# Turning round the two products of every second 128-column block in the channel-major units of a decoder layer

## The chip, the cores and the metric

The kernel runs on one core of one Trainium2 chip, in a single launch. The metric is the device time of one execution in microseconds (us), the median over several runs. The core's engines are named as in the profile: PE is TensorE (its matmuls, here also called products), PEld is TensorE's loading of the stationary operand, DVE is VectorE, ACT is ScalarE, POOL is GpSimd, and SP is SyncE, which issues the weight DMAs.

## What is computed

One decoder layer over 256 tokens of 2048 channels, in float32: half a SwiGLU feed-forward block (FFN1), a mixing stage (sparse attention beside a chunkwise mLSTM, gated and merged), and a second half block (FFN2). Cut to the parts that carry the products:

```python
def swiglu(x, w_gate, w_up, w_down):
    return (jax.nn.silu(x @ w_gate) * (x @ w_up)) @ w_down
...
        x = x + 0.5 * swiglu(rms_norm(x, ffn1_norm[l]), ffn1_w_gate[l], ffn1_w_up[l], ffn1_w_down[l])
        hn = rms_norm(x, mix_norm[l])
        proj = hn @ w_in[l] + b_in[l]
...
        merged = gates[..., :D_MODEL] * (o_nsa @ w_branch_nsa[l]) + gates[..., D_MODEL:] * (h_m @ w_branch_mlstm[l])
        x = x + merged @ w_out[l]
        x = x + 0.5 * swiglu(rms_norm(x, ffn2_norm[l]), ffn2_w_gate[l], ffn2_w_up[l], ffn2_w_down[l])
```

`w_gate` and `w_up` are 2048 x 5632, `w_down` is 5632 x 2048, `w_out` is 2048 x 2048, and the two branch weights are 1024 x 2048.

## The kernel before, in words

The weights stream through once. The program is a list of units (class `Unit`); each is a block of output columns of one weight matrix, cut into tiles of 1024 elements per partition (512 KB). Every tile is loaded by SP into `raw`, ACT casts it to `whi` (float32r, the high part), and DVE subtracts to leave `wlo` (the low part). Four buffers of each kind rotate (`NB = NRAW = 4`); the split of tile h + 3 is issued while tile h is being multiplied (the loop over `plan`, lines 1259 to 1284).

Activations are split likewise. In a channel-major unit (`unit_a`, line 353) the weights are stationary, and the activations of one block of 128 input channels, `a[:, kt]`, move: 256 tokens of the high part and 256 tokens of the low part side by side, 512 columns. For each block `kt` and each `c` of 128 output columns there are two products:

- the high product: `whi` against all 512 columns, into the whole bank `ps[:, c, :]` (line 363);
- the low product: `wlo` against the 256 high columns alone, added to the first half of the same bank (line 364).

A unit has 256 output columns, so `c` is 0 or 1, and a tile holds four `kt`. `kts` is the number of input blocks: 16 where the input has 2048 channels (`XX`, `M_`), 44 in the down projections (`H`), 8 in the branches (`O_`, `h_`). `fold` adds the two halves of the banks afterwards. There are 22 gate and 22 up units in each FFN, 8 and 7 down units in FFN1 and FFN2, and in mixing 24 units of 256 columns on `XX`, one of 128 columns (the gate tile, where `c` is only 0), 8 + 8 branch units and 8 of `w_out`.

Two other kinds of unit are not touched by the change: `unit_b` (token-major, all products of 512 columns, the trace's `mm<-whi,XX` and `mm<-wlo,XX`), and `unit_last` (the last 256 output columns of FFN2, all products of 256 columns). The two `cmp_unit` blocks (`sc<-whi,flat`, `sc<-wlo,flat`) have products of 256 columns as well, 16 in a row for a pair of tiles.

The order of the work on PE is written out by the program itself (a manual schedule): the order of calls is the order of the queue. `Estimate` keeps rough times, from which `step` decides where side work (attention, mLSTM, norms) goes in between the products; `mul` lets some small products of the side work in behind a product of the stream. In the trace nearly all operations carry line L110, that of the helper that passes calls on.

Of the kernel before, what the change touches and what calls it, by code (L numbers as in the profile page):

```python
# [31 lines left out]

# columns of the packed per-partition vectors
C_G1, C_GM, C_G2 = 0, 16, 32
# [11 lines left out]
class Unit:  # L46
    """A weight matrix block that runs through the tensor engine, tile by tile."""

# [5 lines left out]
class Estimate:  # L54
    """Rough times (us) at which the engines get through what they've been given so far, to tell when a
    piece of side work can go into the tensor engine's queue without holding it up."""
    TABLES = {AF.Exp: 1, AF.Silu: 2, AF.Sigmoid: 3, AF.Gelu_apprx_tanh: 4, AF.Ln: 5}
# [5 lines left out]
    def after(self, t):  # L63
        """What follows on the other engines depends on t, and in turn on itself."""
        self.at, self.by, self.end = t, None, t
# [30 lines left out]
class Engine:  # L96
    """Passes calls on, and counts them in the estimate; or keeps them for later (in kept)."""

# [16 lines left out]
def layer(ctx: ExitStack, tc: tile.TileContext, xt, cols, w_small, b_in,  # L115
# [22 lines left out]
    def side_bank(tag):  # L138
        """A bank for side work; free: the times its two banks are given back."""
        est.q["T"] = max(est.q["T"], free[tag].pop(0))  # L140
        held.append(tag)
        free[tag].append(1e9)
        return aux.tile([128, 512], F32, name=nm(tag), tag=tag, bufs=2)
# [4 lines left out]

    # ------------------------------------------------------------------ persistent tiles
    cl = per.tile([128, NCOL], F32, name="cl")  # L150
# [18 lines left out]

    # ------------------------------------------------------------------ helpers  # L170
    def rsqrt(o, ss, n, inv):
        """o = 1/sqrt(ss*inv + EPS), by Newton steps."""
        v = small(n, tag="rv", bufs=2)[0:o.shape[0]]
        t = small(n, tag="rt", bufs=2)[0:o.shape[0]]
        V.tensor_scalar(v, ss, inv, EPS, op0=OP.mult, op1=OP.add)
        V.tensor_scalar(t.bitcast(I32), v.bitcast(I32), 1, None, op0=OP.logical_shift_right)
        V.tensor_scalar(o.bitcast(I32), t.bitcast(I32), -1.0, float(0x5F3759DF), op0=OP.mult, op1=OP.add)
        for _ in range(3):
            V.scalar_tensor_tensor(t, o, -0.5, o, op0=OP.mult, op1=OP.mult)
            V.tensor_mul(t, t, v)  # L180
            V.scalar_tensor_tensor(o, t, 1.5, o, op0=OP.add, op1=OP.mult)

    cur = {}

    # Side work goes in jobs, and these in steps: products first (up to a yield), then what takes
    # them up (up to a yield, of the names of the jobs that have to be over before it goes on, or of the
    # time from which on it can).
    jobs, past = [], {}
# [27 lines left out]
    def step(forced=None):  # L216
        """Starts a step of a job, if one is due; those without products are done at once."""
        while jobs:
# [30 lines left out]
    def mul(*a, **k):  # L249
        """A product of the weight stream; some small ones of the side work go in behind it."""  # L250
        T.matmul(*a, **k)
        for _ in range(min(len(small_ones), 2 + len(small_ones) % 2)):
            small_ones.popleft()()

    def settle():
        """Takes up the small products that were spread over the last ones of the weight stream."""
        while small_ones:
            small_ones.popleft()()
        j, cur["late"] = cur.get("late"), None
        if j:  # L260
            uptake(j)
# [16 lines left out]

    # ------------------------------------------------------------------ weight stream
    tiles = []  # L280
# [54 lines left out]
    def blocks(w, c0, ncol, kts):  # L335
        """The tiles [128, nk, ncol] of 1024 elements per partition of w[:, c0:c0+ncol]."""
        nk = 1024 // ncol
        v = w.rearrange("(k p) n -> p k n", p=128)
        return [(v[:, k:k + nk, c0:c0 + ncol], nk, ncol) for k in range(0, kts, nk)]

    def unit_b(w, c0, H, L, kts, done, pre=None):
        """Token-major: out[tok, 512 columns], activations stationary."""
        def emit(ps, h, e, wh, wl):
# [9 lines left out]
    def unit_a(w, c0, ncol, kts, act, done, pre=None):  # L353
        """Channel-major: out[128 columns, tok] for each 128 of ncol columns, weights stationary."""
        nk = 1024 // ncol

        def emit(ps, h, e, wh, wl):
            a = act()
            for k in range(e * nk // 2, (e + 1) * nk // 2):
                kt = nk * h + k  # L360
                for c in range(ncol // 128):
                    cs = slice(c * 128, c * 128 + 128)
                    mul(ps[:, c, :], wh[:, k, cs], a[:, kt].rearrange("p a t -> p (a t)"), start=kt == 0, stop=False)
                    mul(ps[:, c, 0:S], wl[:, k, cs], a[:, kt, 0, :], start=False, stop=kt == kts - 1)
        return Unit(blocks(w, c0, ncol, kts), emit, done, pre)

    def unit_last(w, c0, ncol, kts, act, done):
        """As unit_a, but with one sum, and one 128 columns after the other at the end; done(ps, c) for each."""
        nk = 1024 // ncol
# [18 lines left out]
    def fold(o, ps, c=2):  # L388
        """Sum of the two halves that unit_a leaves."""
        A.copy(o, ps[:, 0:c, S:])  # L390
# [3 lines left out]

    # ------------------------------------------------------------------ residual stream pieces

    def g_r():
        """rstd of the residual: R per token, and RB along the free axis on each partition."""
        ps = psS()
# [17 lines left out]
    def residual(pool, c, ps, half, gcol, name):  # L417
        """Adds 256 channels to X; then scales and splits them for the next products."""
        y = pool.tile([128, 2, S], F32, name=nm("y"), tag="y", bufs=2)
# [32 lines left out]

    # ------------------------------------------------------------------ FFN
    def ffn(wg, wu, wd, first, nxt, name):
        """first: the job that leaves this norm's rstd; nxt: the next norm's gain column, or None for
        the last one (then it is stored); name: the job that leaves the next rstd."""
        env = {}
# [61 lines left out]

    # ------------------------------------------------------------------ mixing  # L520
    def mixing():
# [50 lines left out]

        # ---- gate tile: rows 0-3 forget, 32-35 input, 64-111 attention gates
        def gate_done(ps):
# [44 lines left out]

        # ---- compressed keys and values  # L620
        def kcvc_done(ps):
# [6 lines left out]
        def g_flat(kc, w):  # L628
            """The blocks' positions on the partitions, split; columns (part, group, block)."""
            tr = psT().rearrange("p (g t) -> p g t", g=2)  # L630
# [9 lines left out]
            for lp in range(2):  # L640
                o = slice(lp * 64, lp * 64 + 64)
                for gpar in range(2):
                    v = tr[gpar * 64:gpar * 64 + 64, :, lp:]
                    # token 16 * block + 2 * k + lp of group 2 * g + gpar
                    src = bass.AP(tensor=v.tensor, offset=v.offset, ap=[v.ap[0], [2, 16], [S, 2], [16, 15]])
# [70 lines left out]

        # ---- queries and keys, normalised
        def normed(src, dst, n):
            """src, dst [128, 2, 64*n/2]: each 64 columns divided by their rms."""
            yield  # L720
# [39 lines left out]
        def g_qt(q, g):  # L760
            """Of each head of the group, both parts of its queries, one below the other."""
            qs = env["q", g] = env["N"].tile([128, 4, S], F32R, name=nm("qs"), tag="qs", bufs=2)
# [15 lines left out]
        def g_kk(g):  # L778
            """The keys of the group (selected, window), split, each part on both halves of the partitions."""
            kk = env["k", g] = env["N"].tile([128, 2, 2, S], F32R, name=nm("kk"), tag="kk", bufs=2)  # L780
# [23 lines left out]

        # ---- attention
        def gates_of(g):
            """Attention gates of the group: [tok, tile, head, branch]."""
            return env["gat"].rearrange("p t (g r b) -> p t g r b", g=4, r=4)[:, :, g]
# [131 lines left out]

        # ---- mLSTM
        def mv_done(c):
# [149 lines left out]

        # ---- merge
        def sig_done(key, c):
# [103 lines left out]

    # ------------------------------------------------------------------ start
    nc.scalar.dma_start(cl, cols)  # L1200
# [55 lines left out]

    # ------------------------------------------------------------------ run
    banks = {}
# [87 lines left out]
```

## Time and profile before

| | us |
|---|---|
| median of 3 runs | 2255.24 (2254.92 to 2256.05) |
| span of the profiled execution, first to last instruction | 2240.6 |
| median less span: what lies around it | 14.6 |
| PE busy | 2228.4 (99%) |
| PEld busy | 1928.6 (86%) |
| DVE busy | 1370.9 (61%) |
| ACT busy | 1105.6 (49%) |
| HBM | 183 GB/s over the span |

The profile gives the profiled execution by its span alone; its 2240.6 us are set beside the median as they stand, and the 14.6 us around it are taken as the same for both kernels. A busy PE is not PE at its peak: a matmul's recorded duration overlaps the next one's. What a product costs is read from the distance between the starts of two products, or from the number of products in a stretch in which PE is never idle; this distance is called the pitch below.

### The profile page before, as it was taken

The page shows a single profiled execution, that of the slowest core. Times are in us where ns is not written, and L with a number is a line of the kernel's source. Part 1 is how long each engine was busy: PE and PEld are TensorE (multiplying, and loading weights), DVE is VectorE, ACT ScalarE, POOL GpSimd, SP SyncE. Part 2 cuts the span into 40 slices and gives each one's busy share as a digit, 9 for nine tenths or more (in the row PEclk, how much of TensorE's full clock was granted, in tenths as well). Part 3 has the DMA queues.
Part 4 walks back from the last instruction along what each step waited for, and adds up shares of the span by engine and source line. Part 5 has one row for each costly group of instructions (what it writes and reads, how often), then busy time and mean ns, then how long its engine had stood idle before and what let it go on. Part 6 is the DMA issues. An engine that isn't in the chain of part 4 may idle for free.

```text
span 2240.6 us, 31889 instructions
## 1 busy us (share of the span) xinstructions
PE 2228.4 (99%) x12685; PEld 1928.6 (86%) x12685; DVE 1370.9 (61%) x1711; ACT 1105.6 (49%) x1471; POOL 27.8 (1%) x54
## 2 busy tenths in 40 slices
PE   9999999999999999999999999999999999999999
PEld 7888888888888888778888888888888888888888
DVE  7656555555555677776766666665555555554553
ACT  6444444444444455566775544554444444443332
POOL 0000000000000000001100000000000000000000
PEclk9999999999999999999999999999999999999999
DMA  7666666666555676444556666655665556565663
GB/s 246 189 190 191 191 188 189 188 188 198 188 189 189 185 238 187 148 123 130 152 163 192 186 187 185 194 182 185 187 186 185 185 185 187 185 195 193 196 196 124
DMA packets 395078, 412.59 MB, mean 184 GB/s; under 512 B 13296, under 2 KB 375920, under 8 KB 394928
## 3 DMA queue, kind: packets, MB, share of 16 engines
q1 hardware_dynamic: 394064, 408.08, 58.9%
q0 software_dynamic: 720, 2.36, 0.4%
q8 instruction: 99, 1.62, 0.3%
q14 instruction: 51, 0.42, 0.1%
q10 hardware_dynamic: 144, 0.11, 0.0%
HBM read 408.40 MB, written 2.10 MB: 183 GB/s over the span
## 4 chain that ended last, share of the span: by engine, by line
PE 97%; DVE 1%; ACT 1%; DMA 1%; issue 0%; SPq 0%; DVEq 0%; ACTq 0%
PE mm L110 94%; PE sc L110 2%; PE tr L110 2%; DVE wlo L110 0%; DMA X<-in_xt_dram 0%; DMA raw<-in_w_in_dram 0%; DVE t L110 0%; DVE nx L110 0%; ACT whi L110 0%; ACT kk L110 0%; ACT t L110 0%; DVE y L110 0%; DVE kk L110 0%; ACT qs L110 0%; ACT XX L110 0%
## 5 line engine op out<-in xcount | busy, mean ns | idle before, releaser
L110 DVE TENSOR_TENSOR wlo<-raw,whi 128x1024 fp32r<-128x1024 f32 (+1 forms) x772 | 929.4, 1224 | 583.4 <-ACT whi L110 580.6
L110 PE MATMUL mm<-XX,whi 128*128 128x512 f32 x3600 | 1269.4, 397 | 4.8 <-DVE XX L110 4.8
L110 ACT CAST whi<-raw 128x1024 fp32r<-128x1024 f32 (+1 forms) x772 | 793.6, 1046 | 581.1 <-PE mm L110 450.1
L110 PE MATMUL mm<-XX,wlo 128*128 128x256 f32 x3600 | 1011.5, 281 | 0.9 <-DVE wlo L110 0.8
L110 PEld LDWEIGHTS mm<-XX,whi 128*128 128x128 f32 x3600 | 676.2, 188 | 165.0 <-ACT whi L110 5.8
L110 PEld LDWEIGHTS mm<-XX,wlo 128*128 128x128 f32 x3600 | 681.2, 189 | 2.7 <-DVE wlo L110 2.5
L110 PE MATMUL mm<-H,whi 128*128 128x512 f32 (+1 forms) x1496 | 493.6, 382 | 0.5 <-DVE y L110 0.5
L110 PE MATMUL mm<-H,wlo 128*128 128x256 f32 x1408 | 395.0, 281 | 0.0
L110 PEld LDWEIGHTS mm<-H,whi 128*128 128x128 f32 x1496 | 274.5, 188 | 58.6 <-DVE y L110 0.7
L110 PEld LDWEIGHTS mm<-H,wlo 128*128 128x128 f32 x1408 | 266.0, 189 | 0.0
L110 PE MATMUL mm<-whi,XX 128*128 128x512 f32 x576 | 192.3, 400 | 0.0
L110 PEld LDWEIGHTS mm<-whi,XX 128*128 128x128 f32 x576 | 108.2, 188 | 21.5 <-issue 0.7
L110 PE MATMUL mm<-wlo,XX 128*128 128x512 f32 x288 | 113.8, 395 | 0.2 <-DVE wlo L110 0.2
L110 PE MATMUL mm<-M__10731,whi 128*128 128x512 f32 x256 | 90.5, 397 | 0.0
L110 PE MATMUL mm<-M__10731,wlo 128*128 128x256 f32 x256 | 71.9, 281 | 0.0
L110 ACT COPY sg<-mm 128x512 f32<-128x512 f32 x44 | 25.8, 587 | 79.8 <-PE mm L110 79.8
L110 ACT COPY sh<-mm 128x512 f32<-128x512 f32 x44 | 25.8, 587 | 78.4 <-PE mm L110 78.4
L110 PEld LDWEIGHTS mm<-wlo,XX 128*128 128x128 f32 x288 | 54.3, 188 | 9.9 <-DVE wlo L110 0.6
L110 DVE TENSOR_TENSOR sg<-mm,sg 128x512 f32<-128x512 f32 x44 | 30.4, 692 | 50.6 <-ACT sg L110 50.5
L110 DVE TENSOR_TENSOR sh<-mm,sh 128x512 f32<-128x512 f32 x44 | 30.4, 692 | 50.2 <-ACT sh L110 50.2
L110 PEld LDWEIGHTS mm<-M__10731,whi 128*128 128x128 f32 x256 | 48.1, 188 | 11.9
L110 ACT CAST H<-sh 128x512 fp32r<-128x512 f32 x44 | 27.3, 621 | 62.1 <-DVE sh L110 62.1
(192 smaller groups left out, 1221.1 us busy)
## 6 DMA issues: line engine op xcount, KB each, us to landing
raw<-in_wu_dram SPq DMA_DIRECT2D x176, 512.0 KB, 4.7
raw<-in_wd_dram SPq DMA_DIRECT2D x176, 512.0 KB, 4.5
raw<-in_wg_dram SPq DMA_DIRECT2D x175, 512.0 KB, 4.7
raw<-in_w_in_dram SPq DMA_DIRECT2D x168, 512.0 KB, 4.4
raw<-in_w_out_dram SPq DMA_DIRECT2D x32, 512.0 KB, 4.5
raw<-in_wb_n_dram SPq DMA_DIRECT2D x16, 512.0 KB, 5.1
raw<-in_wb_m_dram SPq DMA_DIRECT2D x16, 512.0 KB, 4.4
bias<-in_b_in_dram POOLq DMA_DIRECT2D x9, 256.0 KB, 3.7
```

The lines of the kernel that those rows point to most:

```text
L110: return g(out, *a, **k)
```

## The change

In `unit_a`, for odd `c` and for all `kt` but the first and the last of a unit, the low product goes ahead of the high one. The products, their operands and banks are the same; only the order of the two is turned. (The change also drops comments.)

```diff
@@ -360,12 +360,17 @@
                 kt = nk * h + k
                 for c in range(ncol // 128):
                     cs = slice(c * 128, c * 128 + 128)
-                    mul(ps[:, c, :], wh[:, k, cs], a[:, kt].rearrange("p a t -> p (a t)"), start=kt == 0, stop=False)
-                    mul(ps[:, c, 0:S], wl[:, k, cs], a[:, kt, 0, :], start=False, stop=kt == kts - 1)
+                    both = a[:, kt].rearrange("p a t -> p (a t)")
+                    turn = c % 2 == 1 and 0 < kt < kts - 1
+                    if turn:
+                        mul(ps[:, c, 0:S], wl[:, k, cs], a[:, kt, 0, :], start=False, stop=False)
+                    mul(ps[:, c, :], wh[:, k, cs], both, start=kt == 0, stop=False)
+                    if not turn:
+                        mul(ps[:, c, 0:S], wl[:, k, cs], a[:, kt, 0, :], start=False, stop=kt == kts - 1)
         return Unit(blocks(w, c0, ncol, kts), emit, done, pre)
```

On PE, at the border between two tiles in the middle of a gate unit of FFN1 (`mm_380` is the pair of banks of the unit; `whi_362`, `wlo_363` are the old tile, `whi_391`, `wlo_392` the new one), the rows before are:

```order
L110 MATMUL mm_380<-XX,whi_362 128x512
L110 MATMUL mm_380<-XX,wlo_363 128x256
L110 MATMUL mm_380<-XX,whi_362 128x512
L110 MATMUL mm_380<-XX,wlo_363 128x256
L110 MATMUL mm_380<-XX,whi_391 128x512
L110 MATMUL mm_380<-XX,wlo_392 128x256
L110 MATMUL mm_380<-XX,whi_391 128x512
L110 MATMUL mm_380<-XX,wlo_392 128x256
```

and with the change, at the same place:

```order
L110 MATMUL mm_380<-XX,whi_362 128x512 x2
L110 MATMUL mm_380<-XX,wlo_363 128x256 x2
L110 MATMUL mm_380<-XX,whi_362 128x512
L110 MATMUL mm_380<-XX,whi_391 128x512
L110 MATMUL mm_380<-XX,wlo_392 128x256 x2
L110 MATMUL mm_380<-XX,whi_391 128x512 x2
```

The strict alternation of 512 and 256 columns has become two of 512 and two of 256 in turn; the old tile's last product is now one on `whi`, where it was one on `wlo`.

At the border between two units (`mm_482` is the next unit's pair of banks, and `sc_477` a small side product of a norm), the rows before are:

```order
L110 MATMUL mm_380<-XX,whi_391 128x512
L110 MATMUL mm_380<-XX,wlo_392 128x256
L110 MATMUL mm_380<-XX,whi_391 128x512
L110 MATMUL mm_380<-XX,wlo_392 128x256
L110 MATMUL mm_482<-XX,whi_416 128x512
L110 MATMUL sc_477<-ones,acc 128x2 x2
L110 MATMUL mm_482<-XX,wlo_417 128x256
```

and with the change:

```order
L110 MATMUL mm_380<-XX,wlo_392 128x256 x2
L110 MATMUL mm_380<-XX,whi_391 128x512 x2
L110 MATMUL mm_380<-XX,wlo_392 128x256
L110 MATMUL mm_380<-XX,whi_391 128x512
L110 MATMUL mm_380<-XX,wlo_392 128x256
L110 MATMUL mm_482<-XX,whi_416 128x512
L110 MATMUL sc_477<-ones,acc 128x2 x2
L110 MATMUL mm_482<-XX,wlo_417 128x256
```

The last `kt` of one unit and the first of the next keep the old order, four high and four low products that alternate; the side product sits where it sat. On DVE and ACT the sequence of instructions is unchanged.

## Rows read from the trace of the kernel before

**Rows 1.** The page, busy time by engine over the span.
```profile
PE 2228.4 (99%) x12685; PEld 1928.6 (86%) x12685; DVE 1370.9 (61%) x1711; ACT 1105.6 (49%) x1471; POOL 27.8 (1%) x54
```
**Rows 2.** Waits of PE, longest in total: us, times, longest.
```profile
PE mm L110 <- DVE XX L110: 4.8, 1, 4.8
PE mm L110 <- DVE wlo L110: 1.0, 3, 0.5
```
**Rows 3.** Costliest groups: out<-in, form, xcount | busy us, mean ns | idle before.
```profile
L110 PE MATMUL mm<-XX,whi 128*128 128x512 f32 x3600 | 1269.4, 397 | 4.8 <-DVE XX L110 4.8
...
L110 PE MATMUL mm<-H,wlo 128*128 128x256 f32 x1408 | 395.0, 281 | 0.0
```
**Rows 4.** Groups on PE from 60 to 700 us (FFN1).
```profile
L110 PE MATMUL mm<-XX,whi 128*128 128x512 f32 x1268 | 439.6, 391 | 0.0
...
L110 PE MATMUL mm<-H,whi 128*128 128x512 f32 x579 | 200.8, 391 | 0.0
```
**Rows 5.** Groups on PE from 1520 to 2190 us (FFN2).
```profile
L110 PE MATMUL mm<-XX,whi 128*128 128x512 f32 x1321 | 466.8, 399 | 0.0
...
L110 PE MATMUL mm<-H,whi 128*128 128x512 f32 x576 | 203.6, 399 | 0.0
```
**Rows 6.** Groups on PE from 1190 to 1490 us (end of mixing).
```profile
L110 PE MATMUL mm<-XX,whi 128*128 128x512 f32 x386 | 136.7, 399 | 0.0
...
L110 PE MATMUL mm<-M__10731,whi 128*128 128x512 f32 x256 | 90.5, 397 | 0.0
...
L110 PE MATMUL mm<-h__9138,whi 128*128 128x512 f32 x112 | 39.8, 397 | 0.0
L110 PE MATMUL mm<-O__6437,whi 128*128 128x512 f32 x96 | 34.2, 398 | 0.0
```
**Rows 7.** Stretches: busy us (count) of PE, PEld, DVE, ACT, POOL; clock, DMA.
```profile
60.00:700.00 640.00, 640.00 (x3694) 564.32 (x3693) 370.14 (x369) 293.79 (x336) 0.00 (x0) 1.00 0.61 190
1520.00:2190.00 670.00, 670.00 (x3794) 581.00 (x3793) 370.60 (x360) 294.42 (x327) 0.00 (x0) 1.00 0.60 189
```
**Rows 8.** Timeline of PE in a token-major unit: start us, length us, count.
```profile
760.24 0.62 PE L110 MATMUL mm<-whi,XX 128*128 128x512 f32 x2
...
766.37 0.39 PE L110 MATMUL mm<-whi,XX 128*128 128x512 f32 x1
766.60 0.39 PE L110 MATMUL mm<-XX,whi 128*128 128x512 f32 x1
```
**Rows 9.** Timeline of PE around 16 products of 256 columns (mixing).
```profile
803.33 0.39 PE L110 MATMUL mm<-whi,XX 128*128 128x512 f32 x1
803.56 0.28 PE L110 MATMUL sc<-whi,flat 128*128 128x256 f32 x1
803.67 0.28 PE L110 MATMUL sc<-wlo,flat 128*128 128x256 f32 x1
803.79 0.28 PE L110 MATMUL sc<-whi,flat 128*128 128x256 f32 x1
...
805.47 0.40 PE L110 MATMUL mm<-whi,XX 128*128 128x512 f32 x1
805.71 0.40 PE L110 MATMUL mm<-wlo,XX 128*128 128x512 f32 x1
805.94 0.62 PE L110 MATMUL mm<-whi,XX 128*128 128x512 f32 x2
```
**Rows 10.** Timeline of all engines in an up unit of FFN2.
```profile
1800.29 0.28 PE L110 MATMUL mm<-XX,wlo 128*128 128x256 f32 x1
1800.29 0.19 PEld L110 LDWEIGHTS mm<-XX,whi 128*128 128x128 f32 x1
1800.41 0.40 PE L110 MATMUL mm<-XX,whi 128*128 128x512 f32 x1
```
**Rows 11.** Timeline of ACT and DVE there: cast and subtraction of one tile.
```profile
1803.01 1.05 ACT L110 CAST whi<-raw 128x1024 fp32r<-128x1024 f32 x1 [1.77 <-PE mm L110]
...
1804.10 1.23 DVE L110 TENSOR_TENSOR wlo<-raw,whi 128x1024 fp32r<-128x1024 f32 x1 [1.59 <-ACT whi L110]
```

## The prediction

> **What bounds the kernel now.** I read the busy shares first: PE is busy 2228.4 of 2240.6 us, with 12685 products [rows 1]. Then PE's waits: the two longest entries come to 5.8 us in all, nearly all of it one wait at the start [rows 2]. So nothing else holds PE up, and no transfer or cast can be worth more than that. The time is the sum of the pitches of the products, and the question is what a pitch depends on.
>
> For that I count products in stretches where PE is busy for the whole stretch and the granted clock is 1.00 [rows 7]. One high and one low product make a pair. In FFN1, 640 us hold 1268 + 579 = 1847 pairs [rows 4]: 346.5 ns a pair. In FFN2, the same code, 670 us hold 1321 + 576 = 1897 pairs [rows 5]: 353.2 ns. At the end of mixing, 300 us hold 386 + 256 + 112 + 96 = 850 pairs [rows 6]: 352.9 ns. The reader is to see that the same alternation of 512 and 256 columns runs at two pitches 6.7 ns apart, steady over hundreds of us, with no wait, no change of the clock and the same load on the DMAs (190 and 189 GB/s [rows 7]). The longer pitch shows in the recorded length of the 512-column products too (399 against 391 ns [rows 4, 5]).
>
> Uniform runs show what the products cost without alternation. In a token-major unit 28 products of 512 columns lie between the starts 760.24 and 766.60 [rows 8]: 227.1 ns each. From 803.79 to 805.47, 14 products of 256 columns take 1.68 us [rows 9]: 120.0 ns each. Their sum, 347.1 ns, is the pitch of FFN1 within the reading. So **FFN1 runs as the uniform runs do, while FFN2 and most of mixing pay some 6.6 ns a pair on top**. That surplus is what an order of products can win; 0 is the most that it can win in FFN1, where it can only lose.
>
> **The change, part by part.** It adds and removes no product, load, cast or transfer; it moves low products ahead of high ones. I count what it turns. The pairs are 3600 on XX and, for H, the 1408 low products less 88 of the untouched last unit [rows 3], 256 on M [rows 6], and by the loops 128 each in the branches: 5432. A unit turns one pair in each input block but the first and last. The 88 gate and up units and 24 of mixing turn 14 each, 15 down units 42, 8 output units 14, 16 branch units 6: 1568 + 630 + 112 + 96 = 2406. Each turned pair makes a **group of four**, 512, 256, 256, 512: 952 groups in FFN1, 910 in FFN2 and 544 in mixing. A unit's other four pairs stay as they are.
>
> What a group costs today: 2 x 346.5 = 693.0 ns in FFN1, 2 x 353.2 = 706.4 in FFN2, 2 x 352.9 = 705.8 in mixing. What it will cost no row shows in a steady run, so I bound it. The lower end is 693.0, two pairs at FFN1's pitch; the uniform sum is near it, 2 x 227.1 + 2 x 120.0 = 694.2. The upper end is 706.4, FFN2's pitch. The nearest rows are the two switches of length around the 16 short products [rows 9]: the first two of 256 columns after a 512 take 803.79 - 803.56 = 0.23 us, and the first two of 512 after a 256 take 805.94 - 805.47 = 0.47 us, against 0.454 in the uniform run. Together 0.70 us, between the ends; but there each switch follows a long uniform run, and starts are read to 0.01 us. So 694 and 700 both fit; I take the middle, **697 ns**.
>
> By stage, against today: FFN1 952 x (697 - 693.0) = +3.8 us; FFN2 910 x (697 - 706.4) = -8.6 us; mixing 544 x (697 - 705.8) = -4.8 us. The pairs that keep their order at unit borders, four in each of 51 units of FFN2 and 48 of mixing, are 396; if half of them follow their neighbours to the short pitch, they give 198 x 6.5 ns = -1.3 us. The sum is **-10.9 us**, of the span's 2240.6 and likewise of the median, since I take the 14.6 us around the span as fixed: 2255.2 - 10.9 = 2244.3, rounded to 2244.
>
> What else moves. A tile's last reader of whi ends about one low product, 0.12 us, later relative to its neighbour on wlo, and wlo is free about 0.23 us earlier. The cast of a later tile waits for that buffer ("<- PE mm" [rows 11]). Cast and subtraction take 1.05 + 1.23 us [rows 11], and a tile lasts eight pairs, 2.8 us; the split runs three tiles ahead of its use. That leaves about 6 us, so 0.12 us costs nothing; were the cover gone, it would be 0.12 us for each of some 680 tiles, 80 us, and would show as PE waiting on DVE's wlo, 1.0 us today [rows 2]. What wlo is needed for first is unchanged, since the first product pair of a tile keeps its order. Side products sit where they sat, and ACT's and DVE's order is the same.
>
> A weight load starts with the product before its own: 1800.29 for both [rows 10]. So each load is covered by one product, and a 256-column product is the tight cover. In the old order and in the new, half the loads have this cover; that no load loses its cover is why I expect no large loss.
>
> [...]
>
> **The rivals.**
>
> *The order does nothing on balance.* Each stage keeps a pitch that comes from how the stream started after its last disturbance, or the group costs what the two switches add up to, 700 ns: FFN1 +6.7, FFN2 -5.8, mixing -3.2, borders -0.7: -3.0 us, 2252; with the pitches kept, 2255. For it: the same code has two pitches in one execution, so order alone does not decide. Against it: the uniform runs go back to 227.1 and 120.0 after side work, and the new order has two equal neighbours in each group. [...]
>
> *Two short covers in a row.* In the new order two loads in succession have only a 256-column product as cover, where before a 512-column one lay between them. If the surplus of FFN2 comes from the load behind a short product, and the two long products that follow do not take it up, each group pays it twice wherever it runs: 706.4 ns everywhere, so FFN1 loses 952 x 13.4 = +12.8 us, mixing 0.3, and FFN1's border pairs, 52 x 4 x 6.7 ns, 1.4: 2255.2 + 14.5 = 2270. For it: the 512 after a short product is the one that is drawn out, 805.71 - 805.47 = 0.24 us against 0.227. Against it: 14 short covers in a row run at 120.0 ns, without any surplus [rows 9]. Each ns of a group is worth 2406 x 1 ns = 2.4 us, so this case decides from about 703 ns a group on.
>
> *The best case* belongs to the forecast: 693.0 ns in every group, FFN2 -12.2, mixing -7.0, borders -2.6: -21.8 us, 2233.
>
> *The change does not take hold* can be left out: the order of PE's queue, written by hand, shows the groups.
>
> **How the numbers follow.** About 0.2%, 4.5 us, is what a measurement of this kernel can tell from no change. By the 2.4 us a ns, -4.5 us stands at a group of 699.6 ns and +4.5 us at 703.3. The forecast, groups below 699.6, gets 0.54; the balance case, 699.6 to 703.3 or pitches kept, 0.24; two short covers in a row 0.22. So faster 0.54, same 0.24, slower 0.22. The likeliest time is 2244. The range takes in the lower bound, 2234, the balance case, and half of the slow case: up to 2266. The forecast's own range is 2234 to 2251.
>
> **What would show it.** Right: in the changed kernel the stretch of FFN2's units holds its products at about 348.5 ns for a high and a low one, and FFN1's at about the same, a little longer than today; the two FFNs then run at one pitch. PE's waits stay below 10 us in all, the counts of products and loads are those of before, and the casts end as early as now. Wrong in the first way: the two FFNs still differ by 6 to 7 ns a pair, and the start of a stream decides. Wrong in the second way: FFN1 too is at 353 ns or more, with 512-column products of 399 ns. A wait of PE on wlo or whi that was not there would mean that the buffers are freed too late, and my 6 us of slack were wrong. A pitch below 346 ns would mean that the uniform runs are no floor.

## The result, and the profile after

| | before | changed |
|---|---|---|
| median, us | 2255.08 (4 runs, 2254.64 to 2256.05) | 2233.98 (4 runs, 2233.23 to 2235.02) |
| span of the profiled execution, us | 2240.6 | 2233.3 |
| time of the profiled execution, us | not given | 2235.02 |
| ratio of the times | | 0.9912, 95% interval 0.9894 to 0.9931 |

The change wins 21.1 us, 0.9%, about twice the 10.9 that were forecast. The table holds the reason already: the medians lie 21.1 us apart, the two spans only 7.3. Of the changed kernel each run has its span beside its time, and they differ by 1.7 us (2235.02 against 2233.3). Before, I had put 14.6 us there.

The same view of the groups on PE, in the changed kernel, columns as in [rows 3]. First FFN1, from 60 to 700 us:

```profile
L110 PE MATMUL mm<-XX,whi 128*128 128x512 f32 x1272 | 405.8, 396 | 0.0
L110 PE MATMUL mm<-XX,wlo 128*128 128x256 f32 x1272 | 264.0, 279 | 0.0
L110 PE MATMUL mm<-H,whi 128*128 128x512 f32 x563 | 178.0, 396 | 0.0
L110 PE MATMUL mm<-H,wlo 128*128 128x256 f32 x562 | 112.8, 278 | 0.0
```

FFN2, from 1520 to 2180 us:

```profile
L110 PE MATMUL mm<-XX,whi 128*128 128x512 f32 x1325 | 422.5, 396 | 0.0
...
L110 PE MATMUL mm<-H,whi 128*128 128x512 f32 x567 | 179.2, 396 | 0.0
```

The end of mixing, from 1190 to 1480 us:

```profile
L110 PE MATMUL mm<-XX,whi 128*128 128x512 f32 x384 | 122.7, 396 | 0.0
...
L110 PE MATMUL mm<-M__10731,whi 128*128 128x512 f32 x229 | 72.8, 394 | 0.0
...
L110 PE MATMUL mm<-h__9138,whi 128*128 128x512 f32 x123 | 39.8, 394 | 0.0
L110 PE MATMUL mm<-O__6437,whi 128*128 128x512 f32 x96 | 31.4, 397 | 0.0
```

Counted as for the prediction: 640 / (1272 + 563) = 348.8 ns a pair in FFN1, where it was 346.5 [rows 4]; 660 / (1325 + 567) = 348.8 in FFN2, where it was 353.2 [rows 5]; 290 / (384 + 229 + 123 + 96) = 348.6 in mixing, where it was 352.9 [rows 6]. The two FFNs now run at one pitch, and the 512-column products have one recorded length, 396 ns, between the 391 and 399 of before.

The stretches and PE's two longest waits in the changed kernel answer to [rows 7] and [rows 2]:

```profile
60.00:700.00 640.00, 640.00 (x3669) 558.80 (x3668) 369.14 (x368) 292.03 (x335) 0.00 (x0) 1.00 0.61 188
1520.00:2180.00 660.00, 660.00 (x3784) 576.22 (x3783) 371.06 (x360) 293.04 (x326) 0.00 (x0) 1.00 0.61 192
```

```profile
PE mm L110 <- DVE XX L110: 4.8, 1, 4.8
PE mm L110 <- DVE wlo L110: 1.1, 3, 0.5
```

PE is busy throughout both stretches at a granted clock of 1.00, as before, and it waits as little as before. Nothing but the pitch has moved.

The timeline of PE in the middle of a unit of FFN2, changed kernel (start us, length us, count):

```profile
1885.66 0.63 PE L110 MATMUL mm<-XX,whi 128*128 128x512 f32 x2
1886.13 0.39 PE L110 MATMUL mm<-XX,wlo 128*128 128x256 f32 x2
1886.36 0.62 PE L110 MATMUL mm<-XX,whi 128*128 128x512 f32 x2
...
1889.15 0.62 PE L110 MATMUL mm<-XX,whi 128*128 128x512 f32 x2
```

From 1885.66 to 1889.15 there are five groups of four: 698 ns each. Over all 895 groups of FFN2, the starts give 233.2 ns for a 512 after a 256, 233.1 for the 512 after it, 114.9 for the first 256 and 116.3 for the second: 697.5 ns.

To compare kernels I use one more number, worked out from the starts of all products in the trace. A settled uniform run has 226.7 ns for 512 columns and 120.0 for 256; **surplus** is what the products of the channel-major units take beyond that (distances over 24 ns beyond it, where side work or a wait lies between, are left out). Before: FFN1 0.0 us, FFN2 13.2, end of mixing 5.8, the rest 2.4, together 21.4. Changed: 4.6, 4.6, 1.9 and 1.3, together 12.4. So by the profiles the change wins 9.0 us, and 12 us of the result lie outside what the profile of before shows.

### The profile page after: what moved, and what is told of

Its sections match the earlier page's. It is cut to its first block, busy times and chain, and to the rows that moved or that the text cites. A ratio compares the mean times of both kernels' runs of the same rounds, so it can differ in the third digit from the quotient of the medians.

```text
span 2233.3 us, 31888 instructions
## 1 busy us (share of the span) xinstructions
PE 2221.2 (99%) x12685; PEld 1922.6 (86%) x12685; DVE 1371.6 (61%) x1711; ACT 1104.5 (49%) x1471; POOL 27.8 (1%) x54
## 4 chain that ended last, share of the span: by engine, by line
PE 97%; DVE 1%; ACT 1%; DMA 0%; issue 0%; SPq 0%; DVEq 0%; ACTq 0%
PE mm L110 94%; PE sc L110 2%; PE tr L110 2%; DVE wlo L110 0%; DMA raw<-in_wu_dram 0%; DMA raw<-in_w_in_dram 0%; DVE t L110 0%; DVE nx L110 0%; ACT whi L110 0%; ACT kk L110 0%; DVE y L110 0%; ACT t L110 0%; DVE kk L110 0%; ACT qs L110 0%; SPq L295 0%
## 5 line engine op out<-in xcount | busy, mean ns | idle before, releaser
L110 PE MATMUL mm<-XX,whi 128*128 128x512 f32 x3600 | 1158.6, 398 | 4.8 <-DVE XX L110 4.8
L110 PE MATMUL mm<-XX,wlo 128*128 128x256 f32 x3600 | 751.1, 280 | 0.9 <-DVE wlo L110 0.9
L110 PEld LDWEIGHTS mm<-XX,whi 128*128 128x128 f32 x3600 | 569.0, 189 | 26.9 <-ACT whi L110 6.0
L110 PE MATMUL mm<-H,whi 128*128 128x512 f32 (+1 forms) x1496 | 449.0, 383 | 0.5 <-DVE y L110 0.5
L110 PE MATMUL mm<-H,wlo 128*128 128x256 f32 x1408 | 289.7, 279 | 0.0
L110 PEld LDWEIGHTS mm<-H,whi 128*128 128x128 f32 x1496 | 230.5, 189 | 3.5 <-DVE y L110 0.7
L110 PE MATMUL mm<-M__10731,whi 128*128 128x512 f32 x256 | 81.2, 394 | 0.0
L110 ACT ACTIVATE sg<-sg 128x512 f32<-128x512 f32 x44 | 27.8, 632 | 60.2 <-DVE sg L110 60.2
L110 PEld LDWEIGHTS mm<-M__10731,wlo 128*128 128x128 f32 x256 | 48.2, 188 | 9.5
```

The source lines that it names most:

```text
L110: return g(out, *a, **k)
```

## The experiments

Theory A: the profile of before shows an execution that is not the usual one. The alternating order has a short and a long pitch, and which one FFN1 falls into differs from execution to execution; in the usual one, FFN1 too is long. Rival B: the 14.6 us lie around the span.

**The kernel before, executed again.** No edit.

> The kernel before, unchanged, with the span of every execution beside its time. Theory A (the profiled execution of before was not a typical one): the time is the span plus some 1.7 us, as in all four runs of the changed kernel (2235.02 against 2233.3), so a typical execution of before, 2255 us, has a span near 2253.4, and its FFN1 runs at FFN2's pitch, 353.2 ns a pair, where the profile on record has 346.5. Rival B (a fixed 14.6 us lies around the span of before alone): spans near 2240.6 beside times near 2255, and FFN1 at 346.5 ns. By A an execution with FFN1 at 346.5 ns takes about 2242 us.

Twelve executions: four from 2241.22 to 2243.18 us, eight from 2253.87 to 2257.45. Each time is 1.6 to 1.8 us above its own span (2243.18 with 2241.5, 2255.16 with 2253.4). The profiled one took 2243.18 us and has FFN1 short:

```profile
L110 PE MATMUL mm<-XX,whi 128*128 128x512 f32 x1272 | 441.0, 391 | 0.0
...
L110 PE MATMUL mm<-H,whi 128*128 128x512 f32 x575 | 199.4, 391 | 0.0
```

These are its groups from 60 to 700 us; 640 / 1847 = 346.5 ns a pair. Nothing of 14 us lies around the span, so B falls. There are two groups of times 13 us apart, and the profile belongs to the smaller group.

**The kernel before, one more profile.** No edit.

> The kernel before once more, for the profile of one more execution. Theory A: if it takes about 2255 us, its FFN1 runs at 353.2 ns a pair from start to end, everything else as in the profile on record; if it takes about 2242, FFN1 is at 346.5. Rival B: FFN1 at 346.5 ns in an execution of 2255 us.

It took 2242.18 us with a span of 2240.5, and FFN1 was short again (surplus 0.0 us). Over all runs of before in this study, 22 of 80 lie between 2241 and 2245 us and 58 between 2253 and 2259. All three profiles of the kernel before show a short execution; whether that is chance, no run tells, and a profile of a long execution of this very kernel is missing. Two later experiments show FFN1 at the long pitch in kernels that differ from it elsewhere or by a few small products.

**The changed kernel, executed again.** No edit.

> The changed kernel, unchanged, on the chip of the runs beside it. Both theories: 2234 us, a ratio of 0.991 to before. Theory A: every stage at 348.5 to 349 ns a pair in this execution too, and no execution near 2242 or 2255. Rival B says nothing else here.

2233.28 us (six runs, 2232.94 to 2235.01), one group, ratio 0.9918 (0.9893 to 0.9943); the surplus is 12.3 us with the same share in each stage. The span of the profiled execution is 2231.6, so the first profile's 2233.3 was at the upper end; against 2240.6 the spans differ by 7.3 to 9.0 us.

**The turned order in FFN1 alone.**

```diff
-                    turn = c % 2 == 1 and 0 < kt < kts - 1
+                    turn = (w is wg1 or w is wu1 or w is wd1) and c % 2 == 1 and 0 < kt < kts - 1
```

> The turned order in FFN1's three weight matrices alone; everything after FFN1 as before. In 29 executions of before, the times fall in two groups, 8 from 2241.2 to 2244.1 and 21 from 2253.9 to 2258.5 us, some 13 us apart, which is FFN1's 2000 pairs at 6.67 ns. Theory A (the two groups are FFN1's alternation at its short or its long pitch, chosen anew in each execution): with FFN1 in groups of four at 697.5 ns the two groups vanish, and every execution takes 2242.3 + 4.6 = 2247 us, within 2. Rival B (the two groups come from somewhere else in the program): two groups 13 us apart stay.

2246.70 us, ten runs from 2245.34 to 2247.88, in one group, where before on the same chip had five of 23 between 2242.37 and 2243.72 and the others from 2254.37 on; ratio to before 0.9979 (0.996 to 0.9998). FFN1's surplus is 4.6 us, FFN2's 13.2. The two groups of before were FFN1's.

**The turned order everywhere but in FFN1.** The same line with `not` ahead of the bracket.

> The complement: the turned order everywhere but in FFN1, which alternates as before. Theory A: the two groups of times of before are FFN1's alone, so they stay, 13.3 us apart, and lie lower by what the rest wins: FFN2 13.2 - 4.6, the end of mixing 5.8 - 1.8, the middle some 0.7, together 13.3 us: near 2229 and 2242. Rival B: one group.

Ten runs: two at 2229.20 and 2229.58 us, eight from 2241.97 to 2243.85; the median is 2242.13, the ratio to before 0.995 (0.9926 to 0.9973). Two groups, both where they were expected. And this time the profiled execution, 2242.18 us with a span of 2240.5, was one of the longer ones. Its groups from 60 to 700 us:

```profile
L110 PE MATMUL mm<-XX,whi 128*128 128x512 f32 x1268 | 448.1, 399 | 0.0
...
L110 PE MATMUL mm<-H,whi 128*128 128x512 f32 x545 | 192.6, 399 | 0.0
```

640 / (1268 + 545) = 353.0 ns a pair: an FFN1 with the same products in the same order as before, at the long pitch, with the 399 ns of FFN2 [rows 5]. Its surplus is 13.1 us.

**Another disturbance ahead of the alternating stretch.** The small products of the first norm go in together; the weight stream keeps its order from before.

```diff
-SPREAD = ("ca", "R0", "R1", "R2")
+SPREAD = ("ca", "R1", "R2")
```

> The kernel before with one disturbance of FFN1's stream changed: the eight small products of the first norm (near 43 and 49 us) go in together and not spread behind products of the stream. Nothing else of FFN1 is touched. Theory A (what comes before an alternating stretch picks its pitch): the profiled execution has FFN1 from 60 to 700 us at either 346.5 or 353.2 ns a pair, and its time follows, near 2242 or near 2255 us, within 2; the share of executions in either group may differ from that of before (13 of 52 near 2242). Rival B (times and FFN1's pitch have nothing to do with each other): FFN1 at 346.5 in a time near 2255, or at 353.2 near 2242.

All ten runs lie between 2254.89 and 2257.45 us (median 2256.14, ratio 1.0022, 1.0002 to 1.0042); none is short. The profiled execution took 2255.77 us with a span of 2254.1. From 60 to 700 us:

```profile
L110 PE MATMUL mm<-XX,whi 128*128 128x512 f32 x1268 | 448.1, 399 | 0.0
...
L110 PE MATMUL mm<-H,whi 128*128 128x512 f32 x544 | 192.3, 399 | 0.0
```

353.2 ns a pair, and a time near 2255 us, as theory A has it. On PE the edit moves little: the eight products of two columns, two fours around one product of the stream before, stand in a row near 43 us, and four more of the norm stand one product earlier near 49 us; the orders of DVE and ACT differ in a few places from 50 to 62 us. The count alone is weak: on the same chip 15 of 23 executions of before are long, and 58 of 80 in all, so ten long ones in ten would come by chance about once in 70 times by the first share, and once in 25 by the second.

The starts of the products say more. In all three profiles of before the alternation runs at 353 ns a pair from 15 us up to these small products, at 346.7 directly behind the eight, and at 346.7 from 52 us on. With the turned order everywhere but in FFN1 it is the other way round: 346.7 ahead of them, 353.3 from 52 us on. Here the stream comes in at 353 ns, as in the three profiles of before, and from 52 us on it is at 353.3. So the order of the stream does not fix its pitch: it changed at the small products, and by these profiles what it became goes with how the stream came in and with how they stand. For each of the last two cases that is one profile.

**The same lengths with another order of banks.** Both high products of an input block, then both low ones; this makes groups at the borders of a unit too. The diff is cut to the lines that set the order.

```diff
-                for c in range(ncol // 128):
-                    cs = slice(c * 128, c * 128 + 128)
-                    mul(ps[:, c, :], wh[:, k, cs], ...
-                    mul(ps[:, c, 0:S], wl[:, k, cs], ...
+                for c in range(nc_):
+                    mul(ps[:, c, :], wh[:, k, c * 128:c * 128 + 128], both, start=kt == 0, stop=False)
+                for c in reversed(range(nc_)):
+                    mul(ps[:, c, 0:S], wl[:, k, c * 128:c * 128 + 128], a[:, kt, 0, :], start=False, stop=kt == kts - 1)
```

> The same lengths as in the change, 512, 512, 256, 256, but made by taking both high products of an input block and then both low ones, so that it holds in the first and the last block of a unit too, and the bank changes from product to product in another way (0, 1, 1, 0). Theory A, with the surplus hanging on the sequence of lengths alone: 697.5 ns in every group, 2716 groups and no alternating pairs at the borders; the borders of the change pay 4.8 ns a pair against 2.1, 620 pairs, so 1.7 us less than the change: 2232. Rival C (what counts is that two neighbours write the same bank, or that high and low follow each other on one bank): the pitch moves off 348.7 ns a pair by more than 1 ns, to the side of before (353) or of the floor (346.7).

2229.63 us (six runs, 2228.61 to 2230.59), ratio 0.9901 (0.9876 to 0.9926): better than the changed kernel beside it (2233.28) by 3.7 us, where 1.7 were forecast. PE's timeline:

```profile
300.08 0.40 PE L110 MATMUL mm<-XX,wlo 128*128 128x256 f32 x2
300.32 0.63 PE L110 MATMUL mm<-XX,whi 128*128 128x512 f32 x2
...
301.71 0.63 PE L110 MATMUL mm<-XX,whi 128*128 128x512 f32 x2
```

Two groups from 300.32 to 301.71, 0.70 us each; over FFN1 the mean surplus is 3.3 ns a group, against 4.1 inside the units of the change. The rest is the borders, not the banks: in the changed kernel the first group after an alternating border takes 707 ns and the second 694, and from the third on the mean is 696.7 in both FFNs, as much as the 696.7 of the bank order. So rival C falls, and the sequence of lengths is all that shows.

**Runs of eight.** In each half tile all high products, then all low ones, the second half the other way round (diff cut to the lines that set the order).

```diff
+            for low in ((1, 0) if e else (0, 1)):
+                for k, c in ks:
```

> Runs of eight high and eight low products: the high ones of two input blocks, then the low ones of four, and so on. Theory A, with a surplus that belongs to each switch between the lengths: one switch to 512 and back in 16 products instead of four; the 16 short products in the trace of before, with the 512s around them, cost about 18 ns of surplus for the two switches, so some 18 ns for eight pairs, 2.3 ns a pair, or less: 2226 to 2234 us. Rival D (the surplus is what alternation alone locks into, and any run of equal products beyond two is free): below 1 ns a pair, 2224 us. If longer runs hold back the low parts or free the buffers too late, PE waits on wlo or whi appear, and the time goes up.

2232.38 us (2231.95 to 2232.85), ratio 0.9913 (0.9888 to 0.9938). The surplus is 12.7 us, 2.5 ns a pair in the FFNs, so D falls. Longer runs are not better as such. The mean pitches show where it lies: 233.3 ns for the first 512 after a 256, 230.1 for those in the middle, 226.7 for the last; 113.3 for the first 256 after a 512, then 119.9.

**Runs of four.** In each half tile the four high products, then the four low ones (diff cut likewise).

```diff
+            for low in (0, 1):
+                for k, c in ks:
```

> Runs of four: the four high products of two input blocks, then their four low ones. Theory A' (a run of long products pays until it has settled, at +6.7, +8, +2 and +5 ns for the first four after a switch, and the short ones give back 7 to 8 ns in all): 14 ns for four pairs, 3.5 ns a pair, more than with runs of two (1.65 ns a pair, 2229.6) or of eight (2.5): about 2239 us. Rival E (a constant price for each switch, by the runs of two 3.3 ns): 0.8 ns a pair, 2225. Rival F (the price falls evenly between runs of two and of eight): 2 ns a pair, 2231.

2239.91 us (ten runs, 2239.43 to 2240.70), ratio 0.9942 (0.9925 to 0.9958), at the 2239 of A'. PE's timeline:

```profile
300.26 1.09 PE L110 MATMUL mm<-XX,whi 128*128 128x512 f32 x4
301.19 0.64 PE L110 MATMUL mm<-XX,wlo 128*128 128x256 f32 x4
301.67 1.09 PE L110 MATMUL mm<-XX,whi 128*128 128x512 f32 x4
```

Four long products take 0.93 us from 300.26 to 301.19, against 0.907 settled, and four short ones 0.48, as much as settled. Over all of FFN1 the long ones of a run pay 22.6 ns, and the short ones give back 5.9. At 4.1 ns a pair in the FFNs, where A' had 3.5, the runs of four have the largest surplus of the grouped orders, more than twice that of the runs of two. Neither a constant price for a switch nor an even fall holds.

**Runs of sixteen.** All eight high products of a tile, then its eight low ones; the next tile the other way round (diff cut likewise).

```diff
+            low = (e + h) % 2
+            for k in range(nk):
```

> Runs of sixteen: all eight high products of a tile, then all eight low ones, the next tile the other way round. In the trace of the runs of eight, a 512 after a 256 costs 233.3 ns, the next ones 230.1 on average, and the last of the run 226.7; the first 256 after a 512 costs 113.3 and the rest 119.9: about 20 ns for the two switches, in eight pairs. Theory A' (the long products settle within about six, the short ones give back one step of 6.7 ns, and a settled run costs nothing): the same 20 ns for 16 pairs, 1.25 ns a pair, 6.5 us of surplus in all instead of 12.7: 2226 us. Rival D' (the surplus grows with the length of the run): 2.5 ns a pair, 2232. If a longer run of one kind holds back the buffers or shifts the side work, PE waits or changed side work show it.

2230.31 us (2230.11 to 2230.90), ratio 0.9905 (0.988 to 0.993). The surplus came out as A' has it: 1.3 ns a pair in the FFNs, 6.9 us in all. The time did not, 4 us over A'. PE's timeline and its wait on the low parts:

```profile
302.28 2.08 PE L110 MATMUL mm<-XX,wlo 128*128 128x256 f32 x16
304.19 2.00 PE L110 MATMUL mm<-XX,whi 128*128 128x512 f32 x8
```

```profile
PE mm L110 <- DVE wlo L110: 2.9, 4, 1.6
```

Its surplus is 12.7 - 6.9 = 5.8 us below that of the runs of eight, but its time only 2.1. The stretch from 746 to 1185 us, in the runs of sixteen and then in the runs of eight, shows where most of the difference is:

```profile
746.00:1185.00 439.00, 434.55 (x2393) 360.78 (x2392) 325.56 (x624) 275.80 (x501) 24.37 (x36) 1.00 0.54 163
```

```profile
746.00:1185.00 439.00, 436.81 (x2406) 362.66 (x2405) 326.16 (x627) 275.44 (x501) 25.26 (x36) 1.00 0.55 165
```

PE stands idle for 439 - 434.55 = 4.4 us of it, against 439 - 436.81 = 2.2: in mixing, where DVE has side work, PE waits for the subtraction that fills wlo for 1.6 us at 1144.9 and 0.6 us at 1183.4, both ahead of a run of low products. The other 1.5 us or so are not accounted for.

**Runs of sixteen in the FFNs, the bank order in mixing.** The two edits above, chosen by the weight matrix.

> Runs of sixteen in the six FFN matrices, and in the channel-major units of mixing the order with both high products of an input block and then both low ones. Theory A': the FFNs at 1.3 ns a pair over the floor instead of 1.65, mixing as in the runs of two: 1.5 us less than the runs of two everywhere, 2228.1 us against 2229.6. Rival: the wait of PE on wlo that the runs of sixteen had (2.9 us, four times) falls in an FFN, and eats it up: 2230.

2228.36 us (six runs, 2228.10 to 2229.52), ratio 0.9901 (0.9872 to 0.9929), as A' said. The surplus is 7.1 us; the two longest waits of PE for other engines' data are:

```profile
PE mm L110 <- DVE XX L110: 4.8, 1, 4.8
PE mm L110 <- ACT whi L110: 2.0, 2, 1.7
```

The wait on wlo is down to 0.4 us; the one on whi lies in the first 10 us. This kernel has the lowest median of the kernels tried: 5.6 us below the changed kernel as first measured, 1.3 below the bank order alone. Of these two the single times overlap, and they ran on different chips, so the times alone do not show the 1.3; the surplus, some 1.5 us less, agrees with it.

## Why the prediction was right and where it was wrong

*What bounds the kernel.* Right. PE is busy all the time, its waits are those of before, and the whole result is pitch.

*The cost of a group.* Taken at 697 ns between 693.0 and 706.4; measured at 697.5 in both FFNs. That the middle came out is in part luck: 694 and 700 both fitted the starts around the 16 short products [rows 9], and by the finer means of the runs of sixteen the first two long and the first two short products after a uniform run take 233.3 + 235.8 + 113.3 + 119.2 = 701.6 ns. A steady group of four costs 4 ns less than these two switches, which the row did not say.

*The stages.* Against the profile, and with the border pairs counted in, FFN1 was to lose 3.8 us and lost 4.6, FFN2 to win 9.3 and won 8.6, mixing to win 5.4 and won 4.7. The borders were off: I gave the pairs that keep their order half of the way, 1.3 us in FFN2 and mixing and nothing in FFN1. They cost 4.4 ns a pair beyond the settled pitch in both FFNs, against the 6.7 of FFN2 before, so FFN2's won less than half and FFN1's 208 border pairs lost about 0.9 us. Together 9.0 us were won by the surplus, where 10.9 were forecast.

*The step that failed* is "likewise of the median, since I take the 14.6 us around the span as fixed". Some 13 us of these were no time around the span, but FFN1 at the long pitch in the executions that make up the median: 1.7 us are around it, and 2000 pairs x 6.67 ns = 13.3 us are missing from the profile. So for the typical execution FFN1 does not lose 4.6 us by the change but wins 13.1 - 4.6 = 8.5. FFN2 and mixing win 13.5 (the turned order everywhere but in FFN1, medians of the long executions alone: 2255.7 - 2242.2). Together 22.0 us, and 21.1 were measured. That the time came out at 2234, the low end of the range, is luck: that end stood for groups of 693.0 ns, and they took 697.5; what brought the time down there was FFN1. I had written that order "can only lose" in FFN1 and had the same code at two pitches before me; that the pitch could differ between executions too was the conclusion to draw, and a span 14.6 us short of the median was the sign of it.

*The rivals.* "The order does nothing on balance" falls: by the turned order in FFN1 alone and in the rest alone, each part lowers the median by itself (against a short execution the turned FFN1 loses 4.6 us). That a stretch keeps a pitch from its last disturbance, which stood in this rival, fits the alternating order: FFN1 keeps the pitch that it has behind the small products of the norm, in the kernel before, in the rest alone and with the small products together. The grouped orders showed one group of times in every series. "Two short covers in a row" falls: the two short products are the cheap part of a group, 114.9 and 116.3 ns, below the 120.0 of a settled run; what is drawn out are the two long ones, 233 against 226.7 ns.

*The buffers.* Right: PE's wait on wlo is 1.1 us, and was 1.0 [rows 2]. Past the first 60 us only the runs of sixteen come near the end of the cover, with 2.4 of their 2.9 us in mixing.

The Trainium skill ("TensorE: Matmul & The Clock Gate", Back-to-back issue gap) gives N/2.4 + 2.5 ns as the gap of an isolated product of N columns at the full clock, and says of a stream of weight loads and products that both set the spacing. By the formula 512 and 256 columns come to an estimated 215.8 and 109.2 ns. The settled runs here, a load and a product in turn, take longer at both lengths, 226.7 and 120.0 ns, and the neighbours move a pair between 346.7 and 353.3 ns. A product by itself is in none of these runs.

What stays open is the mechanism in the engine. The runs show that surplus follows the sequence of lengths and the history of the stream, that a settled uniform run has none, and that alternation keeps the pitch that it fell into until side products break in, and in FFN1 for 690 us. What sets the pitch of its first 40 us, and why FFN2 was always long, stays open. Why a product after a change of length is drawn out was not tried by itself.

## What to carry to other kernels

Compare the span of a profiled execution with the time of that same execution, and look at all single times before a sum is made against one profile: two groups of times mean that the profile shows one of them. Where a long stream of matmuls is bound by PE alone and alternates between two lengths, count products per microsecond in each stretch; if the same code has two pitches, group equal lengths in twos, or in runs of sixteen, and measure, since the surplus does not fall evenly with the length of a run (two: 1.7 ns a pair, four: 4.1, eight: 2.5, sixteen: 1.3). With FFN1 grouped, the times of a kernel also lie close together: from 2241 to 2259 us before, within 2.6 us in every series with such an order.

## What the runs showed that I had not expected

A strictly alternating stream has two lasting pitches, 346.7 and 353.3 ns a pair, with the granted clock at 1.00 and no wait, and can stay at either for 690 us. In FFN1 the pitch turned at a few small side products, and which one it then kept differs between executions of one program (22 of 80 short), while FFN2 was long in every profile with that order. Settled runs of 512 and of 256 columns, each product with its own weight load, take 226.7 and 120.0 ns: 106.7 ns for 256 columns more, 2.4 columns a ns at a granted clock of 1.00, and 13.3 ns besides for each product. A single change of length is felt for five long products: after sixteen short ones the next took 233.3, 235.8, 228.3, 232.5 and 230.8 ns, and the sixth 226.7; of the short products after long ones the first took 113.3 and the second 119.2 ns, and the third the settled 120.0.
